# The planner of a two-layer hybrid decoder kernel gets other prices and other ranks

## Chip, core and metric

The kernel runs on one core of a Trainium2 chip. The metric is device time in microseconds for one execution of the whole kernel. Times are compared as medians of several runs; a profiled execution has a span (first to last instruction) and a time of its own that is a little longer than the span.

## What is computed

Two decoder layers over 256 tokens of width 1024, all in float32. Each layer has a projection into six blocks of 512 columns, two kinds of attention (eight plain causal heads, four differential heads), an output projection, and a gated feed-forward of width 2816. A conditioning vector c gives shifts, scales and gates for both halves of the layer.

```python
for l in range(DEPTH):
    mod = (cond @ w_mod[l] + b_mod[l])[:, None, :]
    sh_a, sc_a, g_a, sh_f, sc_f, g_f = jnp.split(mod, N_MOD, axis=-1)
    h = rms_norm(x, norm_mix[l]) * (1 + sc_a) + sh_a
    proj = h @ w_in[l]
    mq, mk, mv, dq, dk, dv = jnp.split(proj, splits, axis=-1)
    ...
    x = x + g_a * (jnp.concatenate([o_m, o_d], axis=-1) @ w_out[l])
    h = rms_norm(x, norm_ffn[l]) * (1 + sc_f) + sh_f
    x = x + g_f * ((jax.nn.silu(h @ w_gate[l]) * (h @ w_up[l])) @ w_down[l])
return x
```

The dots leave out the QK norm, the partial rotary embedding, the two attentions and the norm of their heads.

## The kernel before

The 256 tokens are two row tiles of 128. Each dense product in float32 is made of three products in the rounded type fp32r: an operand is split into hi (rounded) and lo (the rest), and `mm3` adds hi x hi, hi x lo and lo x hi into one PSUM tile (L473 to L475). There are 784 such triples of 128x512, 2352 products.

Weights come from HBM into three buffers `raw` of 1 MB by `load_view`; `split` then makes hi on ScalarE (L463) and lo on VectorE (L464), one pair for each half of a buffer, and when lo of both halves is done the buffer is free for the next load. The modulation weights w_mod (8 MB in two sections for the start, 4 MB for each later section) go another way: `mod_section` loads blocks of 512 KB into two buffers `rawm`, and VectorE multiplies each by its column of c and adds it up (L513); after eight blocks the sum is split (L517, L518), TensorE adds it over the partitions with a matrix of ones (L524, L525), and the row goes to SBUF (L530, L533).

The stages follow one another: the start of layer 0 (`start_layer0`: w_mod for shift and scale, of which TensorE takes a part of the blocks in L923 and VectorE the rest in L926, and the first dense products by column blocks as the normalized input becomes known), attention, output projection, `residual` and `norm_modulate` (L566 to L575: scale, shift, transposes L569, hT), feed-forward in 11 chunks (`GateUp`: products, silu and gate L1077 and L1078, transposes L1079, copies L1086 and L1088 into oT; `Down`: product with w_down), then the same for layer 1. The modulation sections of later stages are worked on beside the dense products.

All loads are issued on SP's queue. The order of each engine's instructions isn't written by hand and isn't left to the framework: `Plan` collects every operation with an engine, a cost in ns and its dependencies, and `schedule` simulates the engines and takes, at each step, the instruction that can start first. Among those that can start within a short window of each other on one engine it takes the one with the highest sum of `tail` (the longest path of costs and latencies behind it) and `boost` (a constant of its kind in `TUNE`, plus its rank). `RANK` holds one number for each call of `mark` (each load, split, modulation step, score and so on), times 10 ns. A buffer is given out in the order in which the planner reaches the load. The order so found is emitted as it stands, and on the chip each engine runs its own queue in that order, waiting on semaphores.

The prices that the planner works with are constants of `Plan` and small functions:

- `DMA_ISSUE` 475 ns on SP's queue, `DMA_SETUP` 650, then bytes by `c_dma` at 335 bytes per ns, one load after another, then `DMA_DONE` until an engine can use the data (910 for ScalarE, 1000 for VectorE, 1180 for TensorE).
- `c_sm(n)`, 108 + 1.042 n, for a small VectorE step of n columns, and `SAME`, 127, between dependent steps of VectorE.
- `c_mm(512, 3)`, 3 x 233, for a triple, and `SWITCH`, 85, added to the first triple after other work on TensorE. A transpose costs 109.
- `pe_run` slows TensorE to half speed where the planner believes that it had been idle.

Of the kernel before, what the change touches and what calls it, by code (L numbers as in the profile page):

```python
# [52 lines left out]
class Op:  # L53
    __slots__ = ("eng", "cost", "fn", "deps", "succ", "left", "bufs", "tail", "boost", "idx", "ready", "end", "start", "soft", "main", "group")


class Plan:
# [119 lines left out]
    def schedule(self):  # L177
# [26 lines left out]
        while len(order) < n:  # L204
            best = None
            for e, lst in avail.items():
                cand, tmin = [], 1e18
                for o in lst:
                    t = max(now[e], o.ready)
                    if e == SP:  # L210
                        t = max(t, dma_free - self.AHEAD)
# [45 lines left out]
            if e == SP:  # L257
                now[e] = t + self.DMA_ISSUE
# [39 lines left out]
def c_sm(n):  # L298
    return 108.0 + 1.042 * n


def c_dma(nbytes):
    return nbytes / 335.0
# [13 lines left out]
    "start": (1678,),  # L317
    "smod": (5423, -57, 14, -70, -18, 43, 0, 0, 155, 117, -1394, 257, -1082,),
    "shead": (46, 804, -76, -532, 594,),
    "load": (47, -56, -395, 30, 28, 71, -86, 35, -22, -2708, 746, -967, 12425, 2019, 5536, 3202, 329, 227, -48, 31,  # L320
# [9 lines left out]
    "split": (-691, -30, -11, -339, -5426, 0, -153, -5503, 1328, 0, -571, 1385, 14, 123, -732, -943, -1544, -955,  # L330
# [863 lines left out]
```

## Time and profile before

| | us |
|---|---|
| median of 3 runs | 709.39 |
| lowest, highest | 708.60, 710.76 |
| the profiled execution, its own time | 709.06 |
| its span | 706.9 |
| TensorE busy | 666.8 |
| VectorE busy | 528.5 |
| ScalarE busy | 391.2 |

Busy time of TensorE is the time in which at least one product is under way; products overlap in the pipeline, so the mean duration of one (about 400 ns) is longer than the distance from one to the next (about 232 ns). The busy share is a mean over stages with different limits, so the profile is read by stretches: for each, TensorE's busy time beside its length, the granted clock, and what the other engines and the loads were doing.

### The profile page before, as it was taken

What the parts mean: (1) busy time and instruction counts of PE and PEld (TensorE: products, weight loads), DVE (VectorE), ACT (ScalarE), POOL (GpSimd) and SP (SyncE); (2) the same over time, 40 slices, a digit from 0 to 9 for tenths busy, and PEclk for the clock granted to TensorE, in tenths of its full rate; (3) what the DMA queues carried; (4) which work ended last, traced back from release to release, by engine and by line L of the source; (5) the groups of instructions that cost most, each with busy time, mean ns of one, the idle gap of its engine ahead of it and who ended that gap; (6) DMA issues with size and microseconds to landing.
All of it is one profiled execution on the core that took longest, in us unless ns stands there. A gap on an engine that the chain in (4) does not pass through costs nothing.

```text
span 706.9 us, 8834 instructions
## 1 busy us (share of the span) xinstructions
PE 666.8 (94%) x3085; PEld 520.7 (74%) x3085; DVE 528.5 (75%) x846; ACT 391.2 (55%) x836; POOL 17.0 (2%) x37
## 2 busy tenths in 40 slices
PE   2988999997999999999989999999999999999997
PEld 1656767775778887878768886788788888888885
DVE  3979899999886778787778998996886554464433
ACT  5335899755454544453345766998755444544420
POOL 2000020000000000000000000000000000000000
PEclk9999999999899999999999999999999999999999
DMA  8988885656678679888883589453537555555501
GB/s 267 346 279 296 314 304 178 219 168 227 221 252 284 230 264 313 304 315 295 268 290 134 192 295 318 175 190 110 179 119 249 188 187 194 194 179 178 179 1 59
DMA packets 92496, 158.25 MB, mean 224 GB/s; under 512 B 6030, under 2 KB 62234, under 8 KB 92452
## 3 DMA queue, kind: packets, MB, share of 16 engines
q1 hardware_dynamic: 92452, 157.69, 65.4%
q8 instruction: 24, 0.39, 0.2%
q14 instruction: 20, 0.16, 0.1%
HBM read 156.62 MB, written 1.05 MB: 223 GB/s over the span
## 4 chain that ended last, share of the span: by engine, by line
PE 56%; DMA 14%; issue 12%; DVE 11%; ACT 4%; SPq 1%; POOL 1%; DVEq 0%; ACTq 0%; POOLq 0%
PE ps L475 16%; PE ps L473 16%; PE ps L474 16%; DMA rawm<-in_w_mod_dram 7%; DVE acc L513 4%; DVE lo L464 3%; DMA raw<-in_w_mod_dram 3%; DMA raw<-in_w_in_dram 2%; ACT hi L463 2%; PE ps L674 2%; PE ps L923 1%; PE ps L735 1%; PE ps L1079 1%; ACT w L609 1%; DMA raw<-in_w_down_dram 1%
## 5 line engine op out<-in xcount | busy, mean ns | idle before, releaser
L464 DVE TENSOR_TENSOR lo<-raw,hi 128x1024 fp32r<-128x1024 f32 (+1 forms) x192 | 230.6, 1210 | 99.7 <-ACT hi L463 99.2
L463 ACT ACTIVATE hi<-raw 128x1024 fp32r<-128x1024 f32 (+1 forms) x192 | 198.9, 1050 | 170.8 <-PE ps L475 119.1
L473 PE MATMUL ps<-hi,hThi 128*128 128x512 f32 x544 | 224.0, 412 | 1.9 <-ACT w L609 1.3
L475 PE MATMUL ps<-hi,hTlo 128*128 128x512 f32 x544 | 216.8, 398 | 0.0
L474 PE MATMUL ps<-lo,hThi 128*128 128x512 f32 x544 | 216.5, 398 | 0.0
L473 PEld LDWEIGHTS ps<-hi,hThi 128*128 128x128 f32 x544 | 103.5, 190 | 27.2 <-issue 1.4
L475 PEld LDWEIGHTS ps<-hi,hTlo 128*128 128x128 f32 x544 | 103.0, 189 | 25.6 <-DVE hTlo L951 0.7
L474 PEld LDWEIGHTS ps<-lo,hThi 128*128 128x128 f32 x544 | 103.5, 190 | 24.9 <-issue 1.4
L513 DVE SCALAR_TENSOR_TENSOR acc<-rawm,cs,acc 128x1024 f32<-128x1024 f32 x80 | 102.5, 1281 | 21.5 <-DMA rawm<-in_w_mod_dram 18.7
L473 PE MATMUL ps<-hi,oThi 128*128 128x512 f32 x240 | 96.7, 403 | 3.1 <-ACT oThi L1086 2.3
L474 PE MATMUL ps<-lo,oThi 128*128 128x512 f32 x240 | 95.7, 399 | 1.6 <-DVE lo L464 1.6
L475 PE MATMUL ps<-hi,oTlo 128*128 128x512 f32 x240 | 95.8, 399 | 1.0 <-DVE oTlo L1088 0.8
L473 PEld LDWEIGHTS ps<-hi,oThi 128*128 128x128 f32 x240 | 45.4, 189 | 13.9 <-ACT oThi L1086 2.8
L474 PEld LDWEIGHTS ps<-lo,oThi 128*128 128x128 f32 x240 | 45.4, 189 | 13.4 <-DVE lo L464 3.2
L475 PEld LDWEIGHTS ps<-hi,oTlo 128*128 128x128 f32 x240 | 45.3, 189 | 12.7 <-DVE oTlo L1088 1.2
L692 ACT ACTIVATE w<-ps,sm,sm 128x128 f32<-128x128 f32 (+1 forms) x64 | 32.6, 530 | 7.0 <-DVE sm L687 7.0
L1077 ACT ACTIVATE w<-ps 128x256 f32<-128x256 f32 x44 | 16.7, 382 | 24.0 <-PE ps L475 23.8
L923 PE MATMUL ps<-raw,w 128*128 128x512 f32 (+1 forms) x26 | 14.4, 690 | 14.8 <-DMA raw<-in_w_mod_dram 14.8
L1078 DVE TENSOR_TENSOR w<-w,ps 128x256 f32<-128x256 f32 x44 | 18.1, 416 | 6.1 <-ACT w L1077 6.1
L552 ACT ACTIVATE w<-xs 128x512 f32<-128x512 f32 x16 | 10.0, 627 | 20.9 <-DVE xs L782 19.1
L926 DVE SCALAR_TENSOR_TENSOR acc<-raw,cs,acc 128x512 f32<-128x512 f32 (+1 forms) x27 | 17.0, 630 | 5.6 <-ACT hi L463 4.1
L1086 ACT ACTIVATE oThi<-ps 128x512 fp32r<-128x512 f32 x22 | 12.5, 592 | 15.1 <-PE ps L1079 15.1
(138 smaller groups left out, 593.1 us busy)
## 6 DMA issues: line engine op xcount, KB each, us to landing
rawm<-in_w_mod_dram SPq DMA_DIRECT2D x80, 512.0 KB
raw<-in_w_gate_dram SPq DMA_DIRECT2D x44, 512.0 KB
raw<-in_w_up_dram SPq DMA_DIRECT2D x44, 512.0 KB
raw<-in_w_down_dram SPq DMA_DIRECT2D x22, 1024.0 KB
raw<-in_w_in_dram SPq DMA_DIRECT2D x18, 1024.0 KB
raw<-in_w_mod_dram SPq DMA_DIRECT2D x32, 256.0 KB
raw<-in_w_out_dram SPq DMA_DIRECT2D x8, 1024.0 KB
raw<-in_w_in_dram SPq DMA_DIRECT2D x4, 768.0 KB
```

What stands on the lines that cost most here:

```text
L463: op(ACT, c_act(n, False), lambda: S.activation(hi[:, :n], raw[:, sl], AF.Copy), [raw], [hi], boost=boost)
L464: op(DVE, c_tt(n), lambda: V.tensor_tensor(lo[:, :n], raw[:, sl], hi[:, :n].bitcast(F32), op=ALU.subtract), [raw, hi], [lo], boost=boost)
L473: TE.matmul(ps[:, :], hi[:, k, tt], w[0][:, sl], start=start, stop=False)
L474: TE.matmul(ps[:, :], hi[:, k, tt], w[1][:, sl], start=False, stop=False)
L475: TE.matmul(ps[:, :], lo[:, k, tt], w[0][:, sl], start=False, stop=stop)
L513: op(DVE, c_stt(D), lambda raw=raw, t=t: V.scalar_tensor_tensor(acc[:, :], raw[:, :], cs[:, t : t + 1], acc[:, :], op0=ALU.mult, op1=ALU.a ...
L674: TE.matmul(pss[par][:, c], q, k, start=True, stop=False)
L692: op(ACT, c_act(n, True, 3), lambda ps=ps, pr=pr, j=j, c=c: S.activation(pr[:, j * n : (j + 1) * n], ps[:, j * n : (j + 1) * n], AF.Exp, b ...
L923: op(PE, 4 * W2 / 2.4 + 4.0, lambda r=r, t=t, ps=ps, W2=W2: TE.matmul(ps[:, :W2], cb[:, t * P : (t + 1) * P], r(), start=t == 0, stop=Fals ...
L926: op(DVE, c_stt(W2), lambda r=r, t=t, av=av: V.scalar_tensor_tensor(av(), r(), cs[:, t : t + 1], av(), op0=ALU.mult, op1=ALU.add), rk + [c ...
L1077: last_silu = op(ACT, c_act(FC), lambda: S.activation(sil[:, :FC], ps[:, :FC], AF.Silu), [ps], [sil], after=silu_set, boost=B)
L1078: op(DVE, c_tt(FC), lambda: V.tensor_tensor(sil[:, :FC], sil[:, :FC], ps[:, FC:], op=ALU.mult), [sil, ps], [sil], boost=B)
```

## The change

Prices of the planner change, and all ranks are replaced. What is computed, the instructions, their shapes and the buffers are those of before; `TUNE` is untouched.

```diff
-    SWITCH = 85.0
-    DMA_ISSUE, DMA_SETUP = 475.0, 650.0
-    DMA_DONE = {ACT: 910.0, DVE: 1000.0, POOL: 1000.0, PE: 1180.0, SP: 1000.0}
+    SWITCH = 4.0
+    DMA_ISSUE, POOL_ISSUE, DMA_SETUP = 475.0, 1000.0, 650.0
+    DMA_DONE = {ACT: 1190.0, DVE: 1280.0, POOL: 1280.0, PE: 1460.0, SP: 1280.0}
...
-        if a.eng == SP:
+        if a.dma:
             return self.DMA_DONE[b.eng]
...
-    def op(self, eng, cost, fn, r=(), w=(), after=(), boost=0.0, main=False, rel=0.0):
+    def op(self, eng, cost, fn, r=(), w=(), after=(), boost=0.0, main=False, rel=0.0, dma=False):
         o = Op()
+        o.dma = dma or eng == SP
...
-            if e == SP:
-                now[e] = t + self.DMA_ISSUE
+            if o.dma:
+                now[e] = t + (self.DMA_ISSUE if e == SP else self.POOL_ISSUE)
...
 def c_sm(n):
-    return 108.0 + 1.042 * n
+    return 70.0 + 1.042 * n
...
-def c_dma(nbytes):
-    return nbytes / 335.0
+def c_dma(nbytes, run=4096):
+
+    return nbytes / (317.0 if run >= 1024 else 300.0)
...
 RANK = {
-    "start": (1678,),
-    "smod": (5423, -57, 14, -70, -18, 43, 0, 0, 155, 117, -1394, 257, -1082,),
+    "start": (-248,),
+    "smod": (5813, 213, 3074, 125, -118, 49, -6, 23, 2, 25, -288, 9, 43,),
...
-    def dma(dst, src, nbytes, w, boost=0.0, **kw):
-        return op(SP, c_dma(nbytes), lambda: nc.sync.dma_start(dst(), src, **kw), w=w, boost=boost)
+    def dma(dst, src, nbytes, w, boost=0.0, q=SP, **kw):
+        eng = nc.sync if q == SP else G
+        return op(q, c_dma(nbytes, 4 * src.shape[-1]), lambda: eng.dma_start(dst(), src, **kw), w=w, boost=boost, dma=True)
...
-    def load_view(parts, tag="raw", boost=0.0):
+    def load_view(parts, tag="raw", boost=0.0, q=SP):
```

Every other entry of `RANK` gets a new value in the same manner. The argument `q` can name GpSimd's queue; no call passes it.

## Rows read from the trace of the kernel before

**Rows 1.** The busy line of the page: busy microseconds, share of the span and instructions of each engine.

```profile
PE 666.8 (94%) x3085; PEld 520.7 (74%) x3085; DVE 528.5 (75%) x846; ACT 391.2 (55%) x836; POOL 17.0 (2%) x37
```

**Rows 2.** The table of busy time by stretch. Columns: the stretch in us from the start of the span, its length, busy time (and instructions) of TensorE's matmuls (PE), its weight loads (PEld), VectorE, ScalarE and GpSimd, the granted TensorE clock as a share of full speed, the busy share of the DMA engines and what they moved in GB/s.

```profile
0.00:11.30 11.30, 0.00 (x0) 0.00 (x0) 0.62 (x4) 8.62 (x18) 4.37 (x23) 1.00 0.78 238
11.30:20.00 8.70, 6.12 (x13) 3.82 (x14) 7.20 (x23) 1.90 (x5) 0.00 (x0) 1.00 1.09 334
20.00:46.00 26.00, 26.00 (x96) 17.66 (x96) 23.70 (x49) 7.83 (x12) 0.95 (x1) 1.00 0.94 308
46.00:62.00 16.00, 13.19 (x49) 8.76 (x47) 12.33 (x40) 8.16 (x12) 0.49 (x1) 1.00 0.96 328
62.00:76.00 14.00, 12.09 (x47) 8.87 (x48) 13.96 (x21) 10.36 (x37) 0.46 (x1) 0.88 0.72 251
76.00:96.00 20.00, 17.42 (x81) 13.22 (x80) 16.82 (x49) 18.01 (x96) 0.62 (x3) 1.00 0.92 326
96.00:129.00 33.00, 33.00 (x197) 23.73 (x197) 31.20 (x75) 30.18 (x105) 3.44 (x3) 1.00 0.50 187
129.00:158.00 29.00, 27.60 (x167) 21.87 (x166) 26.23 (x46) 18.98 (x45) 0.96 (x1) 1.00 0.67 222
158.00:181.00 23.00, 16.93 (x73) 12.07 (x72) 22.02 (x37) 10.89 (x20) 0.95 (x1) 0.92 0.68 224
181.00:201.00 20.00, 20.00 (x86) 16.16 (x85) 17.18 (x24) 11.94 (x20) 0.00 (x0) 0.92 0.62 210
201.00:282.00 81.00, 78.66 (x345) 62.68 (x344) 61.46 (x62) 38.34 (x47) 1.85 (x2) 1.00 0.83 278
282.00:360.00 78.00, 78.00 (x345) 62.58 (x344) 59.58 (x59) 32.79 (x40) 1.02 (x2) 1.00 0.86 299
360.00:368.00 8.00, 4.92 (x17) 3.42 (x16) 5.87 (x9) 5.38 (x8) 0.00 (x0) 0.82 0.76 266
368.00:440.00 72.00, 72.00 (x352) 56.38 (x351) 65.16 (x114) 42.90 (x76) 0.96 (x1) 1.00 0.68 237
440.00:512.00 72.00, 70.48 (x395) 56.36 (x394) 61.67 (x126) 64.32 (x204) 0.96 (x1) 1.00 0.49 165
512.00:698.00 186.00, 186.00 (x825) 149.93 (x824) 97.79 (x110) 80.57 (x103) 0.00 (x0) 1.00 0.47 159
698.00:707.00 9.00, 4.39 (x19) 3.19 (x17) 5.71 (x10) 0.00 (x0) 0.00 (x0) 0.97 0.32 117
```

**Rows 3.** The waits of TensorE over the span: line, who was waited for, us in total, times, the longest.

```profile
PE ps L923 <- DMA raw<-in_w_mod_dram: 14.8, 3, 11.4
PE ps L569 <- DVE w L568: 3.1, 3, 1.6
PE ps L473 <- ACT oThi L1086: 2.3, 1, 2.3
```

**Rows 4.** The timeline of TensorE around 48 us: start, duration, what; in brackets the idle time ahead of it and what ended it.

```profile
46.73 0.40 PE L475 MATMUL ps<-hi,hTlo 128*128 128x512 f32 x1
49.38 1.10 PE L923 MATMUL ps<-raw,w 128*128 128x512 f32 x2 [2.26 <-DMA raw<-in_w_mod_dram]
```

**Rows 5.** The timelines of ScalarE and of TensorE around 362 us.

```profile
361.36 1.06 ACT L463 ACTIVATE hi<-raw 128x1024 fp32r<-128x1024 f32 x1 [4.67 <-DMA raw<-in_w_in_dram]
362.32 1.07 ACT L1086 ACTIVATE oThi<-ps 128x512 fp32r<-128x512 f32 x2
...
363.44 0.50 PE L473 MATMUL ps<-hi,oThi 128*128 128x512 f32 x1 [2.33 <-ACT oThi L1086]
...
364.93 0.67 PE L475 MATMUL ps<-hi,oTlo 128*128 128x512 f32 x1 [0.75 <-DVE oTlo L1088]
```

**Rows 6.** The timelines of VectorE and of TensorE ahead of the feed-forward of layer 0.

```profile
169.15 2.60 DVE L513 SCALAR_TENSOR_TENSOR acc<-rawm,cs,acc 128x1024 f32<-128x1024 f32 x2
...
173.07 1.22 DVE L518 TENSOR_TENSOR lo<-acc,hi 128x1024 fp32r<-128x1024 f32 x1
...
174.34 0.50 PE L525 MATMUL ps<-lo,onesr 128*128 128x512 f32 x1 [0.88 <-DVE lo L518]
...
176.85 0.67 PE L569 MATMUL ps<-ident,w 128*128 128x128 f32 x4 [1.55 <-DVE w L568]
```

**Rows 7.** The chain that ended last, in order of time, at a load of 512 KB (rawm) and at one of 1 MB (raw): start, us, what. A DMA's piece goes from the start of its issue to its landing.

```profile
316.82 4.05 DMA rawm<-in_w_mod_dram
...
320.96 1.30 DVE acc L513
...
353.96 7.30 DMA raw<-in_w_in_dram
```

**Rows 8.** The timeline of VectorE in the chain of small steps that works out the rotary angles.

```profile
41.38 0.17 DVE L830 TENSOR_SCALAR kk<-kk 128x16 f32<-128x16 f32 x1
41.59 0.17 DVE L830 TENSOR_SCALAR kp<-kk 128x16 f32<-128x16 f32 x1
```

**Rows 9.** The timeline of TensorE at a change from transposes to dense products.

```profile
75.05 0.63 PE L635 MATMUL ps<-ident,w 128*128 128x128 f32 x4
...
75.76 0.40 PE L474 MATMUL ps<-lo,hThi 128*128 128x512 f32 x1
```

**Rows 10.** The waits of SP's DMA queue, the longest in total.

```profile
SPq L445 <- DVE lo L464: 232.5, 74, 11.7
```

More of the change, by code (lines that the diff above doesn't have):

```diff
@@ L53 @@
 class Op:
-    __slots__ = ("eng", "cost", "fn", "deps", "succ", "left", "bufs", "tail", "boost", "idx", "ready", "end", "start", "soft", "main", "group")
+    __slots__ = ("eng", "cost", "fn", "deps", "succ", "left", "bufs", "tail", "boost", "idx", "ready", "end", "start", "soft", "main", "group", "dma")
 class Plan:
@@ L256, in schedule @@
             now[e] = o.end
-            if e == SP:
-                now[e] = t + self.DMA_ISSUE
+            if o.dma:
+                now[e] = t + (self.DMA_ISSUE if e == SP else self.POOL_ISSUE)
                 o.start = max(dma_free, now[e] + self.DMA_SETUP)
@@ L316 @@
 RANK = {
-    "start": (1678,),
-    "smod": (5423, -57, 14, -70, -18, 43, 0, 0, 155, 117, -1394, 257, -1082,),
-    "shead": (46, 804, -76, -532, 594,),
-    "load": (47, -56, -395, 30, 28, 71, -86, 35, -22, -2708, 746, -967, 12425, 2019, 5536, 3202, 329, 227, -48, 31,
[9 rows of a table removed]
-    "split": (-691, -30, -11, -339, -5426, 0, -153, -5503, 1328, 0, -571, 1385, 14, 123, -732, -943, -1544, -955,
[10 rows of a table removed]
-    "small": (-304,),
-    "qk": (928, 3661, 760, 0, 7233, -353, 4129, 3658, 702, 929, -890, -1288, 9623, 5514, 155, -394,),
@@ L343 @@
-    "values": (1089, -1436, 3482, 0, 1556, -7, -621, 487,),
-    "mod": (10322, 1598, -5442, 198, -193, 816, -230, 5198, 1421, 1919, 283, 2809, -1051, 0, 2321, 7399, 3936, 2059,
[4 rows of a table removed]
-    "modsum": (2277, 4704, 1864, -3911, -443, 4744, -653, -14, 147, 1773,),
-    "score": (4283, 58, -257, -333, -15, -6337, 152, 432, 293, 4213, -4410, -2953,),
-    "prob": (-35, -201, 1641, -113, 1944, 3659, 146, 84, -143, -318, 3, -868, -71, 410, 10714, -23, -45, -58, 902,
-        11377, 0, 1047, -1861, 417,),
-    "rinv": (-1382, 261, 2495, 6769, -10687, 962, 1196, -8714,),
@@ L354 @@
-    "mix": (1272, 3309, 3414, -2657, 816, 105,),
-    "pv": (88, -7274, -1224, 0, -123, 7533, 1679, 4514, 11886, 1854, 1086, 15, -282, 0, 0, 3090, 4491, 79,),
-    "heads": (5698, 3641, -8, 368, 4959, -366, 1408, 2441,),
-    "res": (-213, -587, 117, -103, 9218, 1018, 39, 12, 4975, -3920, -956, -791, 3869, 8797, 1178, 7200,),
-    "xrstd": (-56, 0, 14519, 6442, 1231, -118,),
-    "norm": (819, -246, 1218, -623, 1220, 68, 94, -26, 1575, 582, 2087, 338,),
-    "act": (28, -161, -2267, -1044, -802, -916, -1046, 250, -794, -1883, -4067, -50, -14260, 1668, -3233, -2995, 40,
-        1, 1575, 157, 601, -20, 2292, 86, 468, 1893, -517, 1547, 0, 1044, 1175, -902, -1651, -1853, -245, 7341, 51,
-        -3985, 135, -1337, 0, 42, -5464, -5439,),
@@ L363 @@
-    "aT": (4485, 534, -10757, -2641, -1038, -13578, -1638, 473, -6665, 3494, 59, -2558, 418, -2716, -28, -248, 4611,
-        84, -1742, -4170, 1329, -4036,),
+    "start": (-248,),
+    "smod": (5813, 213, 3074, 125, -118, 49, -6, 23, 2, 25, -288, 9, 43,),
+    "shead": (283, 209, 311, -884, 748,),
+    "load": (2488, 5618, 321, 3574, -272, -6, -16, 4487, 0, -22, 483, -494, -16, -57, -324, 98, 154, 185, 38, 96,
[9 rows of a table added]
+    "split": (-3533, -218, 102, -5748, 769, -2824, -5328, -1257, 857, -4222, 1064, -174, 2440, 135, -811, -5217,
[10 rows of a table added]
@@ new lines @@
+    "small": (871,),
+    "qk": (-35, 1954, -85, 18, 15, -219, 2316, 1451, 100, 102, 430, 7387, 1339, -3, 6502, 1497,),
+    "values": (202, 51, -177, 1313, -368, -430, 9117, 3485,),
+    "mod": (6906, 1964, 4710, -860, 120, -1031, 75, 4770, 257, -341, 4972, 30, 447, 4370, 983, 1521, 1783, -206,
[4 rows of a table added]
+    "modsum": (170, 24, 401, -2450, 3247, 4421, -168, -28, -350, 2257,),
+    "score": (2969, -22, -36, 154, 45, -1373, 85, -93, 302, 1237, 3040, -27,),
+    "prob": (-268, 132, -14, 51, -13, 33, -15, 48, -30, -29, -71, -45, -1307, -353, 1745, -841, -144, -150, 5590,
+        736, -288, 408, 1597, -30,),
@@ new lines @@
+    "rinv": (918, -352, 3806, 166, 3655, -3767, 108, 350,),
+    "mix": (7838, 402, 776, -61, 3603, 2320,),
+    "pv": (4, 191, -101, 564, 1427, 3028, 68, 3751, 7239, 698, 2207, -519, 61, 5530, 0, 4246, 6054, 5933,),
+    "heads": (-13, -34, 53, -7, 562, 1708, 3223, 604,),
+    "res": (87, 53, 434, 16, 3796, -1654, -57, 3, 3103, 14268, -406, -491, 530, -1238, -2020, -194,),
+    "xrstd": (16, 157, -6554, 3884, 2621, -149,),
+    "norm": (15163, 650, 204, 0, 0, 0, 3761, -243, 2948, 2739, 4574, 3681,),
@@ L365 @@
+    "act": (-118, 179, 1116, -1229, 4936, 6541, -74, -1137, 430, 3540, 2566, -7642, 3669, 1372, 2779, 255, -955,
[4 rows of a table added]
 }
@@ L454, in load_view @@
         for key, view, src, nbytes in parts:
-            dma(lambda view=view: view(raw.tile), src, nbytes, [(raw, key)], boost=boost)
+            dma(lambda view=view: view(raw.tile), src, nbytes, [(raw, key)], boost=boost, q=q)
         return raw
```

50 rows, old and new, of the table RANK are left out of this document.

## The prediction

> **What bounds the kernel now.** I read the busy line of the page first: TensorE is busy 666.8 us (94% of the span of 706.9), VectorE 528.5 [rows 1]. So TensorE bounds the whole, and as the change adds and removes no instruction, the most that a new order could win is the 40.1 us in which TensorE stands still, plus what it loses at the lower clock.
>
> The table of busy time by stretch says where those microseconds lie [rows 2]. The reader should look at three columns in each row: TensorE's busy time against the length, the granted clock, and whether VectorE or the load stream is full in the same stretch. Three long stretches show TensorE busy all the time at clock 1.00: 282 to 360, 368 to 440 and 512 to 698, together 336 us; nothing is to be won there. The first 20 us lose 13.9 (11.3 + 2.6) before and between the first loads, and the last 9 lose 4.6 behind the last product; I count both as fixed. What is left is a pool of short stalls:
>
> (a) 46 to 76: 2.81 + 1.91 idle, and the clock of 0.88 over 14 us costs 0.12 x 14 = 1.7: 6.4 in all.
> (b) 76 to 96: 2.58 idle.
> (c) 129 to 201: 1.40 + 6.07 idle, and 0.92 over 23 and over 20 us costs 1.8 + 1.6: 10.9.
> (d) 201 to 282 and 440 to 512: 2.34 + 1.52 = 3.9 idle, thinly spread over 153 us.
> (e) 360 to 368: 3.08 idle, and 0.82 over 8 us costs 1.4: 4.5.
>
> The pool is 28.3 us. The clock's two levels are 2.4 and 1.2 GHz; the stretches below 1.00 are those in which TensorE had just stood still, so their loss goes when the stall goes.
>
> Then the waits of TensorE, for what ended each stall, and the timeline around the three largest. The waits name a load (14.8 us, 11.4 of it the very first), the normalized rows w of L568, and oThi of L1086 [rows 3]. In (a) the last dense product before the gap starts at 46.73 and the next work waits 2.26 us for a block of w_mod [rows 4], while the stream already runs at 308 to 328 GB/s [rows 2]. In (e) ScalarE reaches the split of a w_in load before its bytes are there, stands 4.67 us, and the copy L1086 that TensorE needs is queued behind it: TensorE waits 2.33 and then 0.75 [rows 5]. In (c) VectorE is busy 22.02 of 23 us; two modulation sums L513 and the split L518 lie ahead of the row of shifts, and TensorE's transposes L569 wait 1.55 us for it [rows 6].
>
> **The change, part by part.** No duration on the chip is altered: prices only decide in which order the planner writes each engine's queue and which buffer a load gets. So each price is worth what its error did to the order.
>
> Loads. The old price of a 512 KB load that waits for its buffer is 475 issue + 650 setup + 524288/335 = 1565 + 1000 until VectorE: 3.69 us. The new one is 475 + 650 + 1654 + 1280 = 4.06. The trace has such a load start at 316.82 and VectorE start on it at 320.96: 4.14 [rows 7]. The new price is 0.08 short, the old 0.45. For 1 MB into ScalarE the old sum is 475 + 650 + 3130 + 910 = 5.17, the new 5.62; the w_in load of (e) took 7.30 from 353.96 [rows 7], behind others. So the new price closes 0.46 of an error of 2.1. In the start it is the rate that counts: 238 x 11.3 + 334 x 8.7 + 308 x 26 = 13.6 MB by 46 us [rows 2]; that is 40.6 us at 335 bytes per ns and 42.9 at 317. The difference, 2.3, is the size of the 2.26 us stall at 49.38. So the old planner did not see that stall and the new one does.
>
> One rule of the Trainium skill speaks against the higher load price: DMA: Bandwidth & Descriptors, section "Anatomy of one DMA", puts the fixed part of a load on GpSimd's path at about 2.0 us. With 1.65 for 512 KB at 317 that would be 3.65, the old price, and the raise would only put work off. The 4.14 us of [rows 7] stand against it.
>
> Small VectorE steps. Their price for 16 columns falls from 108 + 17 = 125 to 87 ns, with 127 between dependent ones: 252 before, 214 now. The chain of the rotary angles starts a step every 0.21 us [rows 8]. The new price fits within 4 ns. It frees 38 ns a step in the plan and nothing on the chip; where VectorE is full, as in (c), the planner now sees some room that it did not use.
>
> First dense product after other work (SWITCH 85 to 4). Four transposes at 109 and one product at 233 are 669 ns; with 85 it is 754, with 4 it is 673. The trace has 0.71 us from the first transpose at 75.05 to the second product at 75.76 [rows 9]: 0.04 over the new price, 0.04 under the old. Nothing hangs on it.
>
> The choice of a GpSimd queue for loads has no caller that passes it; every load stays on SP's queue, so GpSimd's queue is not used more and its issue price of 1000 ns is idle. Cost nil, and no cover is needed.
>
> The new ranks are the part without a row: they change nearly every choice between ready instructions. I bound them by stage. Nothing recovered is 0; everything recovered is the pool; and in the three full stretches they can only lose. One late load there costs what it costs in (e), 4.5 us with its clock.
>
> What I take: (a) 2.0 of 6.4: the bytes are the same and the stream is full until 62 us, so only work that the load does not hold can move into the gap. (b) 0.5 of 2.6: loads at 326 GB/s and ScalarE at 18.0 of 20 both hold [rows 2]. (c) 2.5 of 10.9: VectorE has only 1.8 + 2.8 + 1.0 = 5.6 us of idle between 96 and 181 [rows 2], and about half of that should be usable, since its sums wait on loads that are now priced right. (d) 0.5 of 3.9. (e) 2.0 of 4.5, for the reason that the mispriced load is its cause, though the price closes only a part. New stalls in the full stretches: 1.5 lost. Sum: -2.0 - 0.5 - 2.5 - 0.5 - 2.0 + 1.5 = -6.0. The profiled execution took 709.06 (span 706.9 and 2.16 around it), 0.33 under the median of 709.39; 709.06 - 6.0 = 703.1, or 703.4 as a median. Late after the change: in (a) the same load stream, in (c) VectorE, so neither goes to zero.
>
> **The rivals.** First, no change: the limits in (a) to (c) are a full load stream and a full VectorE, which no order widens. The stalls then move, and (d) and (e) give about 1 us that new ones take back: 709. For it: 22.02 of 23 and 328 GB/s. Against: the full stretches show that the planner can keep TensorE fed wherever its prices hold, and (e) is not such a limit. Chance 0.16.
>
> Second, slower, by the raw buffers. Believing in later loads, the planner ranks other work ahead of the splits; ScalarE and VectorE then take a landed load later, its buffer comes free later, and the next load is issued later: SP's queue already waits 232.5 us in total for VectorE's L464 to free a buffer [rows 10]. In the layer-0 feed-forward (201 to 360) the stream runs at 278 and 299 GB/s [rows 2], so a slip is not caught up at once and ends as a stall like (e). The terms (a) to (e) give 7.5; two such stalls (9.0) outweigh them, and that is the point from which it decides; three make 13.5 - 7.5 = +6: 715. For it: only three raw buffers. Against: VectorE is busy just 61.5 of 81 and 59.6 of 78 us there, so splits need not wait long. Chance 0.15.
>
> Third, much more: with stalls seen in advance, half the pool goes and none is added: 709.06 - 14 = 695. For it: each stall is short and other dense work follows within 1 to 3 us. Against: (c). Chance 0.10.
>
> Fourth, the higher load price is wrong: then (a) and (e) give nothing, 709.06 - 3.5 + 1.5 = 707.1. A load of 3.7 us in a quiet stream would show it; the nearest I have is 4.14. Chance 0.05. By the rule of the Trainium skill's page DMA: Bandwidth & Descriptors this would be the outcome.
>
> **How the numbers follow.** A measurement of this kernel can tell about 0.3%, so "the same" is 707.3 to 711.5. My forecast, 698 to 707.3 with 703 as the likeliest, has 0.54. With the third rival, faster has 0.64. The first and the fourth make 0.21 for the same, and slower is 0.15. The range for 8 in 10 leaves out half of the third rival below and most of the second above: 696 to 712.
>
> **What would show it.** Right: at 360 to 368 ScalarE no longer stands in front of L1086 and the clock stays at 1.00 there; the gap before 49.38 is shorter than 1 us or has dense products in it; 158 to 201 stays at clock 1.00 while VectorE is still over 95% busy; the three full stretches stay full. Wrong: TensorE's idle time (40.1 us) is the same or more with stalls at new places, above all with a raw load as releaser between 201 and 360; or the start is shortened by far more than 2 us, which would mean that it was not the load stream that held it.

## The result, and the profile after

The changed kernel took 699.3 us (median of 4 runs, 698.36 to 700.71), the kernel before 710.08 beside it (4 runs, 708.6 to 711.08). The ratio is 0.9851, with a 95% interval of 0.9825 to 0.9878. The forecast was 703.0, with a range of 696 to 712. The profiled execution of after took 698.36 with a span of 696.2, against 709.06 and 706.9 before: 10.7 us less on either. The lines named here stand three lower than before (L473 to L475 are L476 to L478 now).

The busy line of the page of after (answers to [rows 1]):

```profile
PE 663.0 (95%) x3085; PEld 519.3 (75%) x3085; DVE 528.1 (76%) x846; ACT 391.5 (56%) x836; POOL 16.8 (2%) x37
```

The instructions are the same in number on every engine, and the busy time of VectorE and ScalarE has hardly moved. TensorE's busy time fell by 3.8 us (666.8 to 663.0) with the same 3085 instructions, and its idle time from 40.1 to 33.2 (696.2 - 663.0).

The table of busy time by stretch of after (answers to [rows 2], same columns; the stretches past 350 are set by after's own stages):

```profile
46.00:62.00 16.00, 15.65 (x63) 10.80 (x62) 13.60 (x39) 7.64 (x12) 0.95 (x1) 1.00 1.02 370
62.00:76.00 14.00, 13.25 (x58) 10.25 (x57) 13.60 (x31) 12.31 (x63) 0.00 (x0) 1.00 0.74 248
76.00:96.00 20.00, 19.52 (x110) 15.02 (x109) 18.49 (x50) 18.22 (x75) 2.87 (x4) 1.00 0.99 347
96.00:129.00 33.00, 29.21 (x160) 20.97 (x158) 30.71 (x72) 27.04 (x94) 0.95 (x1) 0.90 0.56 189
...
158.00:181.00 23.00, 18.31 (x73) 13.26 (x72) 21.98 (x35) 11.32 (x22) 0.95 (x1) 0.93 0.65 229
181.00:201.00 20.00, 20.00 (x92) 16.19 (x91) 19.18 (x27) 11.92 (x17) 0.00 (x0) 1.00 0.69 225
201.00:282.00 81.00, 80.46 (x356) 64.23 (x355) 64.62 (x64) 38.04 (x46) 1.91 (x2) 1.00 0.86 296
282.00:350.00 68.00, 67.61 (x296) 53.79 (x295) 51.80 (x52) 30.61 (x37) 0.95 (x1) 1.00 0.86 300
350.00:360.00 10.00, 10.00 (x48) 8.06 (x47) 8.66 (x11) 6.58 (x9) 0.00 (x0) 1.00 0.88 320
360.00:430.00 70.00, 70.00 (x335) 55.93 (x334) 61.21 (x111) 43.86 (x74) 1.91 (x2) 1.00 0.62 206
...
502.00:688.00 186.00, 186.00 (x825) 149.85 (x825) 97.54 (x110) 80.92 (x103) 0.00 (x0) 1.00 0.47 159
```

TensorE's column is now almost full in 46 to 96, and the place of the old stall (e) is full at clock 1.00. But one stretch that was full before, 96 to 129, has lost 3.8 us and some clock.

The waits of TensorE in after, over the span (answers to [rows 3]):

```profile
PE ps L926 <- DMA raw<-in_w_mod_dram: 11.3, 1, 11.3
PE ps L931 <- DVE acc L929: 4.3, 2, 3.9
PE ps L572 <- DVE w L571: 3.2, 3, 1.7
PE ps L638 <- ACT w L630: 1.8, 1, 1.8
PE ps L527 <- ACT w L630: 1.2, 1, 1.2
```

TensorE waits for a load once instead of three times, 11.3 us instead of 14.8, and the wait for oThi is gone. In the start VectorE's sums took over: TensorE waits 4.3 us for acc of L929, so that at the first dense product after is only 0.6 us ahead. It waits for the rows w of L571 as before (3.2 and 3.1 us): that is the full VectorE of (c). New are two waits for ScalarE's w of L630, in attention. The timeline of TensorE there (start, duration, then in brackets the idle time before it and its releaser):

```profile
106.30 0.50 PE L527 MATMUL ps<-hi,onesr 128*128 128x512 f32 x1 [1.20 <-ACT w L630]
...
108.85 1.12 PE L638 MATMUL ps<-ident,w 128*128 128x128 f32 x4 [1.81 <-ACT w L630]
...
110.74 0.79 PE L476 MATMUL ps<-hi,hThi 128*128 128x512 f32 x1 [0.78 <-ACT qkT L641]
```

ScalarE works there through the 16 short squares of the keys' norm (L612, about 0.2 us each) while the PSUM tiles of the keys are held, and TensorE has no other tile to go on with: 1.20 + 1.81 + 0.78 = 3.8 us idle. The clock falls behind it:

```profile
107.70:114.53 6.83, 4.91 (x16) 3.82 (x16) 6.50 (x14) 4.73 (x17) 0.00 (x0) 0.50 0.34 103
```

The planner knew of this stall. The schedule that the planner of after makes (model times) has TensorE idle there for 1.19, 2.05 and 0.94 us, 4.2 in all, between the triples 79 and 80; only the clock at half speed isn't in it. The two stalls of before at 49.38 and in (e) are of the other kind: the old planner's schedule has no idle time of TensorE over 0.3 us there, while the stalls of (c) are in it, with up to 1.85 us each.

ScalarE and SP's queue at the former stall (e), timeline of after (answers to [rows 5]; first ScalarE, then two loads of w_in, and the second of them by itself):

```profile
353.24 1.06 ACT L466 ACTIVATE hi<-raw 128x1024 fp32r<-128x1024 f32 x1 [1.73 <-PE ps L478]
354.20 0.58 ACT L1089 ACTIVATE oThi<-ps 128x512 fp32r<-128x512 f32 x1
...
356.55 0.59 ACT L1089 ACTIVATE oThi<-ps 128x512 fp32r<-128x512 f32 x1
357.03 1.06 ACT L466 ACTIVATE hi<-raw 128x1024 fp32r<-128x1024 f32 x1
```

```profile
344.54 3.02 SPq L448 DMA_DIRECT2D raw<-in_w_in_dram  x2
...
347.19 0.38 SPq L448 DMA_DIRECT2D raw<-in_w_in_dram  x1
```

The split that stood in front of the copies before is the one at 357.03 here, and its load is the second of the two: by the order in which the kernel emits loads and splits, the one at 344.54 belongs to the split at 353.24. So the load that was issued at 353.96 before [rows 7] is issued at 347.19. The split between the copies finds its bytes there, and no L1089 stands behind a load.

Where the 10.7 us came from can be counted by the dense triples, which run in one fixed sequence in both kernels. The start of a triple's first product, before and after (other work of TensorE can move across such a mark, so a part is good to about 1 us; between the marks 96 and 150 a second profiled execution of after, that of after_again, takes 1.6 us longer than this one):

```
triple      0      48     64     80     96     150    200    350    376    392    520    783
before   22.36  75.44  89.96 110.77 136.71 197.98 235.32 347.38 372.17 384.25 510.48 701.53
after    21.78  71.94  85.25 110.74 136.86 194.41 230.76 343.24 362.34 374.52 499.87 690.87
diff     -0.58  -3.49  -4.70  -0.03  +0.15  -3.57  -4.56  -4.14  -9.82  -9.73 -10.61 -10.67
```

So (a) gave 3.5 us (0.6 of it ahead of the first triple), (b) 1.2, the new stall in attention cost 4.85 (from -4.70 to +0.15), (c) gave 3.7 (to triple 150; 2.1 by after_again), (e) 5.6 (from -4.14 to -9.73), and the stretches of (d) 0.6 and 0.9.

### The profile page after: what moved, and what is told of

It is laid out like the page before. It is cut to its first block, busy times and chain, and to the rows that moved or that the text cites. A ratio compares the mean times of both kernels' runs of the same rounds, so it can differ in the third digit from the quotient of the medians.

```text
span 696.2 us, 8830 instructions
## 1 busy us (share of the span) xinstructions
PE 663.0 (95%) x3085; PEld 519.3 (75%) x3085; DVE 528.1 (76%) x846; ACT 391.5 (56%) x836; POOL 16.8 (2%) x37
## 4 chain that ended last, share of the span: by engine, by line
PE 64%; DMA 14%; DVE 12%; ACT 6%; issue 2%; SPq 1%; POOL 0%; DVEq 0%; ACTq 0%; POOLq 0%
PE ps L477 19%; PE ps L478 19%; PE ps L476 19%; DMA rawm<-in_w_mod_dram 6%; DMA raw<-in_w_mod_dram 3%; DVE acc L516 3%; DVE lo L467 3%; PE ps L738 2%; ACT hi L466 1%; ACT w L612 1%; DMA raw<-in_w_in_dram 1%; DVE acc L929 1%; PE ps L677 1%; PE ps L1082 1%; DMA raw<-in_w_out_dram 1%
## 5 line engine op out<-in xcount | busy, mean ns | idle before, releaser
L467 DVE TENSOR_TENSOR lo<-raw,hi 128x1024 fp32r<-128x1024 f32 x192 | 230.7, 1210 | 97.8 <-ACT hi L466 96.9
L466 ACT ACTIVATE hi<-raw 128x1024 fp32r<-128x1024 f32 x192 | 199.1, 1052 | 153.3 <-PE ps L478 111.9
L476 PE MATMUL ps<-hi,hThi 128*128 128x512 f32 x544 | 222.9, 410 | 1.9 <-ACT hThi L952 1.2
L478 PE MATMUL ps<-hi,hTlo 128*128 128x512 f32 x544 | 216.8, 398 | 0.1
L476 PEld LDWEIGHTS ps<-hi,hThi 128*128 128x128 f32 x544 | 103.2, 190 | 26.9 <-ACT hThi L952 1.7
L478 PEld LDWEIGHTS ps<-hi,hTlo 128*128 128x128 f32 x544 | 103.0, 189 | 24.8 <-DVE hTlo L954 0.5
L476 PE MATMUL ps<-hi,oThi 128*128 128x512 f32 x240 | 97.3, 405 | 1.5 <-ACT oThi L769 0.8
L478 PE MATMUL ps<-hi,oTlo 128*128 128x512 f32 x240 | 95.2, 397 | 0.3 <-DVE oTlo L771 0.3
L476 PEld LDWEIGHTS ps<-hi,oThi 128*128 128x128 f32 x240 | 45.2, 188 | 11.6 <-ACT oThi L769 1.0
L478 PEld LDWEIGHTS ps<-hi,oTlo 128*128 128x128 f32 x240 | 45.1, 188 | 11.3 <-DVE oTlo L771 0.7
L926 PE MATMUL ps<-raw,w 128*128 128x512 f32 (+1 forms) x26 | 13.4, 646 | 11.3 <-DMA raw<-in_w_mod_dram 11.3
L929 DVE SCALAR_TENSOR_TENSOR acc<-raw,cs,acc 128x512 f32<-128x512 f32 (+1 forms) x27 | 16.9, 631 | 5.0 <-DMA raw<-in_w_mod_dram 4.4
L677 PE MATMUL ps<-qkT,qkT 64*128 64x128 f32 (+1 forms) x128 | 19.1, 375 | 0.5 <-ACT qkT L641 0.5
```

The source lines that it names most:

```text
L466: op(ACT, c_act(n, False), lambda: S.activation(hi[:, :n], raw[:, sl], AF.Copy), [raw], [hi], boost=boost)
L467: op(DVE, c_tt(n), lambda: V.tensor_tensor(lo[:, :n], raw[:, sl], hi[:, :n].bitcast(F32), op=ALU.subtract), [raw, hi], [lo], boost=boost)
L476: TE.matmul(ps[:, :], hi[:, k, tt], w[0][:, sl], start=start, stop=False)
L478: TE.matmul(ps[:, :], lo[:, k, tt], w[0][:, sl], start=False, stop=stop)
L677: TE.matmul(pss[par][:, c], q, k, start=True, stop=False)
L929: op(DVE, c_stt(W2), lambda r=r, t=t, av=av: V.scalar_tensor_tensor(av(), r(), cs[:, t : t + 1], av(), op0=ALU.mult, op1=ALU.add), rk + [c ...
```

## The experiments

The theory, called L in the expectations, from the profile: the old planner believed loads to be there sooner than they are, so its order ran into stalls that it didn't see; with the new load prices the search sees and removes them, and the load prices do most of the work. The rivals: that any long new search would do as well, whatever the prices; that the small steps and SWITCH do it; and, beside these, that the new load price isn't the duration of a load at all (the prediction's fourth rival).

Except in the two load tests the whole reference is computed. New ranks of my own come from a random search: change some ranks, make the planner's order again, keep it if the planner's end falls. Each is the outcome of one such search; how far two searches with the same prices differ was not measured.

**1. loads_alone.** It leaves out the whole computation and only loads. One buffer is loaded and read, then loaded again; then streams with nothing to wait for, in rows of 4 KB, 2 KB, 1 KB and 512 B.

```diff
+            for t in range(KT):
+                nc.sync.dma_start(one[:, :1024], wm[:, t, s * D : (s + 1) * D])
+                V.scalar_tensor_tensor(acc[:, :], one[:, :1024], cs[:, t : t + 1], acc[:, :], op0=ALU.mult, op1=ALU.add)
+        for k in range(10):
+            ...
+            nc.sync.dma_start(one[:, :].rearrange("p (a b) -> p a b", b=512), wi[:, 4 * g : 4 * g + 4, ...])
+            S.activation(hi[:, :], one[:, :], AF.Copy)
```

> Leaves out the whole computation; it only loads weights. Part 1 loads 512 KB into one buffer, which VectorE reads before the next load; part 2 the same with 1 MB and ScalarE; part 3 streams 8 MB each in rows of 4 KB, 2 KB, 1 KB and 512 bytes with nothing to wait for. By the new prices a 512 KB load lies between two VectorE steps for 475 + 650 + 1654 + 1280 = 4.06 us and a 1 MB load between two ScalarE steps for 5.62 us, and the streams run at 317 GB/s (300 for 512 bytes). By the old prices 3.69 and 5.17 us, and 335 GB/s for all. By the Trainium skill's page DMA: Bandwidth & Descriptors, section Anatomy of one DMA, the fixed part would be 2.0 us, and so 512 KB 3.6 us (an estimate with the rate of the stream).

The timeline of VectorE and ScalarE in it: the bracket is the whole time from the end of one read, which frees the buffer, to the start of the next.

```profile
12.71 1.28 DVE L88 SCALAR_TENSOR_TENSOR acc<-one,cs,acc 128x1024 f32<-128x1024 f32 x1 [3.39 <-DMA one<-in_w_mod_dram]
17.41 1.28 DVE L88 SCALAR_TENSOR_TENSOR acc<-one,cs,acc 128x1024 f32<-128x1024 f32 x1 [3.42 <-DMA one<-in_w_mod_dram]
...
100.69 1.91 ACT L93 ACTIVATE hi<-one 128x2048 fp32r<-128x2048 f32 x1 [5.08 <-DMA one<-in_w_in_dram]
107.70 1.91 ACT L93 ACTIVATE hi<-one 128x2048 fp32r<-128x2048 f32 x1 [5.10 <-DMA one<-in_w_in_dram]
```

The table by stretch for the four streams (columns here: stretch, length, VectorE, ScalarE, GpSimd, clock, DMA share, GB/s):

```profile
151.00:166.00 15.00, 0.00 (x0) 1.14 (x1) 0.00 (x0) 1.00 1.03 410
168.00:185.00 17.00, 0.18 (x1) 0.00 (x0) 0.00 (x0) 1.00 1.05 389
187.00:206.00 19.00, 0.35 (x2) 0.00 (x0) 0.00 (x0) 1.00 0.88 293
208.00:240.00 32.00, 0.35 (x2) 0.00 (x0) 0.00 (x0) 1.00 1.03 282
```

A lone load of 512 KB takes 3.4 us from free buffer to VectorE, one of 1 MB 5.1 us to ScalarE. The old prices say 3.69 and 5.17, the new ones 4.06 and 5.62: for a load by itself the old prices are the nearer. From first to last packet the streams run at 403, 369, 337 and 286 GB/s (the table's stretches lie inside the streams, but the third begins before its stream). 524288 bytes at 403 bytes per ns are 1.3 us, which leaves 2.1 us fixed. The fixed part of about 2.0 us in the Trainium skill (DMA: Bandwidth & Descriptors, "Anatomy of one DMA") agrees with this, though the page gives it for GpSimd's path and these loads are on SP's queue.

**2. loads_busy.** It leaves out the computation too: the same serial loads of 512 KB while nothing else, ScalarE, VectorE, TensorE or all three work without pause, then two streams beside all three.

```diff
+        for busy in ((0, 0, 0), (1, 0, 0), (0, 1, 0), (0, 0, 1), (1, 1, 1)):
+            phase(*busy, 34.0, serial)      # 8 loads into one buffer
+        phase(1, 1, 1, 28.0, rows4k)
+        phase(1, 1, 1, 30.0, rows1k)
```

> Leaves out the whole computation. Eight loads of 512 KB follow one another into one buffer, in five phases: alone; while ScalarE copies 128x1024 tiles without a break; while VectorE subtracts such tiles; while TensorE multiplies; with all three. Then 8 MB stream in rows of 4 KB and of 1 KB with all three at work. If busy engines slow the loads, the distance from load to load rises from about 3.4 us towards the 4.06 of the new price and the streams fall from 404 and 342 GB/s to about 320. If they don't, all stays as alone (within 0.1 us and 3%), and the late loads of the whole kernel come from loads queued behind each other.

SP's queue in it (start of the first issue, time to the end of the last of eight), while ScalarE, VectorE, TensorE and all three work:

```profile
33.74 25.38 SPq L96 DMA_DIRECT2D one<-in_w_mod_dram  x8
...
62.36 25.44 SPq L96 DMA_DIRECT2D one<-in_w_mod_dram  x8
...
90.94 26.01 SPq L96 DMA_DIRECT2D one<-in_w_mod_dram  x8
...
120.17 25.32 SPq L96 DMA_DIRECT2D one<-in_w_mod_dram  x8
```

Less the last issue itself (0.33), seven spacings in 25.32 to 26.01 us are 3.57 to 3.67 us each, whichever engine works; in the quiet phase, once the loads ahead of it are done, they are 3.45 to 3.59. In the last phase ScalarE joins only at 128.20, behind the third issue; the spacings from there on are 3.49 to 3.61. The stream of 4 KB rows still issues a load every 1.28 us beside three busy engines (524288 / 1.28 = 410 bytes per ns). So busy engines make a load some 0.1 us longer at most in the mean. In the whole kernel loads are late where other loads are ahead of them. Of the rawm loads of before for which VectorE stood still, one issued at 147.01, 1.8 us behind another rawm load, reached VectorE 4.85 us later; two issued at 322.27 and 416.09, 3.2 and 2.3 us behind a raw load, 5.60 and 5.48; one at 129.70, 1.3 us behind a raw load, 6.10; and one at 289.87, with two raw loads less than 3 us ahead, 7.60. With nothing issued in the 5 us ahead the trace of before has this one, 3.28 us from issue to VectorE:

```profile
230.60 0.34 SPq L445 DMA_DIRECT2D rawm<-in_w_mod_dram  x1
...
233.88 1.28 DVE L513 SCALAR_TENSOR_TENSOR acc<-rawm,cs,acc 128x1024 f32<-128x1024 f32 x1 [1.04 <-DMA rawm<-in_w_mod_dram]
```

After has another at 472.08: 3.30 us. The 4.14 us of [rows 7], on which the prediction leaned, was thus not a quiet load: a raw load had been issued 4.6 us ahead of it. The new price of 4.06 us is a quiet load and some 0.7 us more.

**3. swap_one_split.** The kernel before, with nothing but the w_in split of (e) moved behind the copies that were queued behind it, on ScalarE and VectorE.

```diff
+    late = [o for o in order if o.group == ("split", 102) and o.eng != PE]
+    last = next(o for o in order if o.group == ("aT", 10) and o.eng == DVE)
+    order = [o for o in order if o not in late]
+    at = order.index(last) + 1
+    order[at:at] = late
```

> The kernel before with one change: one half-split of a layer-1 w_in load (ScalarE's copy and VectorE's rest) is emitted behind the copies L1086 and L1088 of the last feed-forward chunk of layer 0 instead of ahead of them. If the stall at 360 to 368 comes from that split standing in front of L1086 while its load is late, TensorE's waits of 2.33 and 0.75 us and the lower clock (1.4 us) go: 4.5 us less, ratio about 0.9935. If the triples there would wait for another thing as well, or the time comes back in layer 1, the ratio is 0.998 to 1.002.

707.57 us (12 runs) against 709.12 (23 runs); ratio 0.9989, 0.9961 to 1.0016. ScalarE's timeline there, the stretch of (e) and the one after it, and what TensorE waited for in the latter:

```profile
352.81 1.09 ACT L1086 ACTIVATE oThi<-ps 128x512 fp32r<-128x512 f32 x2 [3.11 <-PE ps L1079]
...
357.33 2.00 ACT L463 ACTIVATE hi<-raw 128x1024 fp32r<-128x1024 f32 x2
```

```profile
356.00:364.00 8.00, 6.88 (x31) 5.30 (x31) 5.81 (x6) 3.31 (x4) 0.00 (x0) 1.00 0.64 218
364.00:384.00 20.00, 18.75 (x85) 14.85 (x84) 18.42 (x32) 11.86 (x22) 0.00 (x0) 1.00 0.52 180
```

```profile
372.37 0.66 PE L569 MATMUL ps<-ident,w 128*128 128x128 f32 x4 [1.25 <-DVE w L568]
```

The stall did go: the copies run first, the clock stays at 1.00, and from triple 350 to 376 the profiled execution gains 3.65 us on that of before. By triple 392 it has given back 1.5: TensorE waits 1.25 us for VectorE's rows w of L568, while no product waits for the moved split. (This execution, 700.78 us, is the fastest of the twelve, and 5.95 us ahead of before already at triple 350, which the change doesn't touch.) Over the whole run no gain is shown clear of noise, and 0.9935 lies outside the interval. After did something else: against the triples around it the load is issued 2.6 us earlier and ScalarE reaches the split 4.5 us later.

**4. new_prices_old_ranks and old_prices_new_ranks.** One part of the change each.

```diff
 RANK = {
-    "start": (-248,),
+    "start": (1678,),
...
```

(all ranks of before under the new prices; the other kernel is the reverse, the kernel before with after's `RANK`).

> All new prices, ranks of before. Theory L (the gain comes from ranks that were found with prices at which late loads are seen): no gain, since these ranks were fitted to other prices; 706 to 716 us. Theory P (right prices put the work in a better order by themselves): most of the gain, 699 to 705 us.

> All old prices, the new ranks. Theory L: the ranks fit the prices with which they were found, and are worse than nothing without them; 715 us or more, since nearly every choice is then another one. Theory S (the new ranks are better numbers, whatever the prices): 699 to 705 us.

New prices with old ranks: 710.87 us (10 runs), ratio 1.002 (0.999 to 1.005). Old prices with new ranks: 746.32 us (4 runs), 1.0521 (1.0478 to 1.0565). Both came out as theory L expected, and neither part alone gives anything. Ranks are offsets to a choice that the prices make; these were worth something only under the prices they came with.

**5. search_all_new, search_load_price, search_small_and_switch.** My own search, 60,000 trials from the ranks of before, under all the new prices, the new load prices alone, and the new small-step and SWITCH prices alone. The same search under all old prices found nothing better than the 691.6 that the old planner gives before's order (model time; there is no run of it).

```diff
 RANK = {
-    "start": (1678,),
+    "start": (28179,),
...
```

> All new prices; ranks from a search of my own that starts at the ranks of before (60,000 trials). Replayed with the new prices its order ends at 694.4 us, with the old ones at 706.2; the order of before ends at 705.1 with the new and 691.6 with the old ones. Theory L (the new prices, the load's above all, tell the chip's time of an order): 1.8 to 8 us over 694.4 as seen in the two known traces, and 2.1 around the span: 698 to 705 us, a gain. If the old prices were the right ones: about 14 us slower than before, 723 us.

> Only the load prices are new (SWITCH 85 and the small-step price as before); ranks from the same search with the same number of trials, from the ranks of before. Replayed with all new prices its order ends at 702.9 us, with the old ones at 705.7. Theory L: 707 to 713 us, about as before, since the search had got no further than this order; if the old prices were right, 722 us. A time under 705 would say that the load price alone carries the gain.

> Only the small-step price and SWITCH are new, the load prices are those of before; ranks from the same search with the same number of trials. The planner that made it expects 698.2 us; replayed with all new prices the order ends at 717.6, with the old ones at 708.0. Theory L: the loads come later than this planner thinks, 721 to 728 us, slower than before and the slowest of the three. If the load price doesn't matter, it is as fast as the search with all new prices, 698 to 705 us.

All new prices: 704.79 us (7 runs) against 709.6 (22 runs), ratio 0.9931 (0.9883 to 0.9979). Load prices alone: 711.95, 1.0043 (1.0015 to 1.007). Small steps and SWITCH alone: 715.11, 1.0076 (1.0041 to 1.011). The first lies in the range that theory L gave it, and so does the second; the third is the slowest, as expected, but not as slow as its range (721 to 728). A search of the same length under all three prices does gain, 0.7%. That the load prices do most of the work isn't shown: alone they are slower than before, by 0.4%, and the small steps and SWITCH alone too. This part of the theory falls.

**6. after_again, search_further, search_late_loads.** On one chip: after itself; its ranks searched on for 48,000 trials with the planner's end as the goal; and its ranks searched for another goal (some 178,000 trials): the mean end of six replays of the order in which each load comes late by a random time (0.5 us in the mean, at most 1.5) and the phase of the planner's model of the slow clock is shifted. Only `RANK` differs.

```diff
 RANK = {
-    "start": (-248,),
+    "start": (6729,),
...
```

(that of search_late_loads; search_further has 14511.)

> The changed kernel as it is, timed again beside the next two on one chip. Its order ends at 688.2 us in the planner; if each load lands late by a random part of 1.5 us (mean 0.5) and the clock's phase is shifted, the mean of six replays is 705.1. Measured before: 699.3.

> The ranks after, searched further with the same prices and the same goal (the planner's end, 48,000 trials): 687.9 us in the planner, 702.1 as the mean of the six replays with late loads. If the planner's end tells the chip's time to a few tenths, 699.0 us; if what is left is how an order bears late loads, 696 to 700 us.

> The ranks after, searched with the same prices but another goal: the mean of the six replays in which each load lands late by a random part of 1.5 us. The planner's end is 688.0 us, as good as the search further; the mean of the replays is 691.6, 10.5 less. Theory L carried further (what costs time on the chip is loads that land later than planned, and orders differ in how they bear it): 692 to 697 us, clearly under the other two. If prices alone matter: 699 us, the same as the search further.

Against 708.31 us for before (7 runs): after 698.76, 0.9859 (0.9818 to 0.99); search_further 698.12, 0.9854 (0.9821 to 0.9886); search_late_loads 693.07, 0.9783 (0.9746 to 0.9821). More search for the planner's end brings nothing. The search for orders that bear late loads brings another 5.7 us (693.07 against 698.76), though its planned end, 688.0, is that of after, 688.2, within 0.2. Its busy line and two stretches:

```profile
PE 659.1 (95%) x3085; PEld 519.2 (75%) x3085; DVE 528.9 (77%) x846; ACT 391.8 (57%) x836; POOL 16.2 (2%) x37
```

```profile
96.00:129.00 33.00, 32.58 (x190) 24.17 (x189) 31.54 (x72) 28.86 (x99) 0.95 (x1) 1.00 0.64 214
...
282.00:360.00 78.00, 78.00 (x348) 62.88 (x347) 61.95 (x63) 36.45 (x46) 0.95 (x1) 1.00 0.87 295
```

Attention (96 to 129) is almost full again, at clock 1.00: the stall that after had newly made is not there. Half of what this kernel gains over before is busy time of TensorE, 666.8 to 659.1.

**7. old_prices_late_loads.** The same goal under all old prices (some 183,000 trials from the ranks of before): the kernel before with another `RANK`, nothing else.

```diff
 RANK = {
-    "start": (1678,),
+    "start": (29669,),
...
```

> All prices of before; ranks searched from those of before with the goal of the late loads (the mean of six replays in which each load lands late by a random part of 1.5 us). With the old prices its order ends at 692.0 us, 0.4 later than the order of before (691.6). Replayed with the new prices it ends at 696.0, where the order of before ends at 705.1. If late loads are what costs time, and an order that bears them will do without right prices: 700 to 706 us, a gain of 4 to 9. If right prices are needed: 708 to 711 us, as before.

692.89 us (4 runs) against 708.66 (7 runs), ratio 0.9792 (0.9732 to 0.9852): as fast as search_late_loads, and below every number that was expected of it. So the new prices are not needed for a gain of this size. Its busy line, the waits of TensorE, and those of VectorE and ScalarE for loads:

```profile
PE 660.6 (96%) x3085; PEld 518.4 (75%) x3085; DVE 526.9 (76%) x846; ACT 390.9 (57%) x836; POOL 16.7 (2%) x37
```

```profile
PE ps L896 <- DMA raw<-in_w_mod_dram: 12.8, 3, 10.9
PE ps L446 <- ACT w L582: 1.6, 1, 1.6
```

```profile
ACT hi L436 <- DMA raw<-in_w_up_dram: 28.4, 15, 3.6
...
DVE acc L486 <- DMA rawm<-in_w_mod_dram: 18.6, 21, 3.2
```

VectorE still stands 21 times for a rawm load, 18.6 us in all, exactly the count of before (21 times, 18.7), and the longest wait is longer. Yet past the start TensorE has no wait for a load among its largest. So VectorE finds its loads late as often as before, and TensorE hardly stands for it; that other work is ready for it then is my reading, which no run tests by itself.

The planner's replay puts the orders side by side. Each order is kept as it was emitted and simulated with either set of prices, and with the new prices and late loads (mean of six replays); these three are model times (the random draws are others than those behind the figures in the expectations), the last column is the chip's median.

```
order                      old prices  new prices  new + late   chip
before                        691.6       705.1       722.1     708.3 to 710.1
after                         700.4       688.2       705.2     699.3
new_prices_old_ranks          714.8       705.2       718.0     710.9
old_prices_new_ranks          740.5       753.6       766.5     746.3
search_all_new                706.2       694.4       707.2     704.8
search_load_price             705.7       702.9       716.3     712.0
search_small_and_switch       708.0       717.6       732.6     715.1
search_further                698.8       687.9       703.9     698.1
search_late_loads             695.7       688.0       692.7     693.1
old_prices_late_loads         692.0       696.0       705.4     692.9
```

Read down the first column: the old planner calls before's order the best of all, and after's 8.8 us longer. The second column puts most of the kernels in the chip's order. With old prices the replay of before's order is at 355.35 us when triple 376 starts, with new prices at 369.35; the chip has 372.17. But this doesn't show that the new prices are the better ones: the first column does as well once before's own row is left out, and it has after at 700.4 (chip 699.3), search_all_new at 706.2 (704.8) and search_further at 698.8 (698.1), where the new prices have 688.2, 694.4 and 687.9. What falls short by 10 to 18 us is the end that a planner gives to an order that was searched for that very end: before by the old prices, those three by the new ones, and search_small_and_switch, 698.2 by its own prices and 715.1 on the chip. Such a search picks, among others, the orders about which its prices are too hopeful; a goal with random lateness leaves less of that. This fits all rows but search_load_price (705.5 by its own prices, 712.0); no run tests it by itself. The last row is in line with it: 696.0 by the new prices, more than after's 688.2, and 692.9 on the chip, less than after's 699.3. For before's order the load prices alone give 707.7 in the replay, where all new prices give 705.1 and all old ones 691.6; the small steps alone give 692.6, SWITCH alone 690.5. The loads are the part that matters in the replay.

## Why the prediction was right, and where its sizes were off

The direction and the bound were right: the gain came out of the pool of short stalls (40.1 us idle before, 33.2 after), the stretches from 282 on that were full stayed full but for 0.39 us, and nothing in the instructions changed. The predicted time is 3.7 us above the measured one and the range holds it. Term by term:

| term | predicted | measured | |
|---|---|---|---|
| (a) 46 to 76 | -2.0 | -3.5 | idle 4.72 to 1.10, clock 1.00; 0.6 of it lies ahead of the first triple |
| (b) 76 to 96 | -0.5 | -1.2 | idle 2.58 to 0.48, at 347 GB/s instead of 326 |
| (c) 129 to 201 | -2.5 | -3.7 | TensorE still waits for w of L571, 2.5 us there; -2.1 by after_again |
| (d) | -0.5 | -1.5 | |
| (e) | -2.0 | -5.6 | the whole stall and its clock |
| new stalls | +1.5 | +4.85 | in attention, not in a stretch that was counted; +4.1 by after_again |
| sum | -6.0 | -10.65 | |

**The step that was mis-sized most is (e).** It took 2.0 of 4.5 because "the price closes only a part": 0.46 of an error of 2.1 us. That reasoning treats a price as if it repaired its own error in place. But the new order doesn't shift the load by the change of its price. Counted from triple 350, the load is issued 2.6 us earlier (347.19 against 353.96, in a kernel that runs 4.1 us ahead there) and ScalarE reaches the split 4.5 us later, 7.1 us in all where 4.67 were missing; so this stall went whole. The error of a price is thus no bound on what a new order wins. swap_one_split shows the other half: removing this stall by hand gives part of it back 16 triples later.

**New stalls** were put in the three full stretches, at 1.5. Those held. The fourth full stretch, 96 to 129 [rows 2], was left out of the list, and there it cost 4.85 us. The mechanism is not that of the second rival: no raw load is the releaser, ScalarE's short steps of the keys' norm are. Nor is it an error of a price: the planner has these 4.2 us of idle time in its own schedule, and the order was kept with them for an earlier end. What it doesn't have is the 6.8 us at half speed behind them, in which TensorE worked for 4.91 us and so lost some 2.5 (an estimate); its schedule of after has triple 80 at 108.29 and triple 96 at 132.46, the chip at 110.74 and 136.86.

**The loads' paragraph** argued that the new price fits (4.06 against 4.14). As a duration of a load by itself this is wrong: 3.4 us. The fourth rival's sign, a load of 3.7 us or less in a quiet stream, stood in the trace of before (3.28 us at 230.60), so that "the nearest I have is 4.14" misread it. The rival's result, 707.1, did not follow. That the price works as an allowance for loads queued behind other loads would explain it, but no run shows it: with the load prices alone the search gained nothing (711.95). The rule of the Trainium skill that was weighed there (DMA: Bandwidth & Descriptors, "Anatomy of one DMA") agrees with the 3.4 us; what was drawn from it for the time of the kernel fell with that rival.

**Signs.** That the stall at 49.38 and that of (e) were unseen by the old planner and went is the part of the mechanism that the traces show; that the load price is what made them go is not shown, since neither half of the change gains alone, nor do the load prices alone, nor the other two. As forecast: ScalarE no longer stands in front of the copies and the clock is 1.00 there; the stall before 49.38 is gone (0.35 us idle in 46 to 62); VectorE is over 95% busy in 158 to 181 (21.98 of 23); the three full stretches stayed full. Not as forecast: 158 to 181 is still at clock 0.93, only 181 to 201 is at 1.00; the start gained 3.5 where about 2 was expected, while the stream ran faster in the same stretch (370 GB/s instead of 328 in 46 to 62), so part of the room there was in the order of the loads and not in the rate of the stream.

**Open.** Whether the late loads or the shifted phase of the clock in the goal makes the last 6 us isn't separated. Nor is it from the number of trials, three times that of the plain searches; only search_further, which stopped gaining, speaks against that. The goal's lateness adds 0.5 us to a load in the mean, so that a 512 KB load at old prices has 3.69 + 0.5 = 4.19 us in it, about the new price: that a spread does more than one raised price is likely from search_late_loads against search_further, but wasn't tried with a fixed 0.5. Why search_load_price is slower than before, with the part that counts most in the replay, is not explained.

The best version is 693 us (search_late_loads, old_prices_late_loads), 2.1 to 2.2% under before and 0.8 to 0.9% under after.

## What to carry to other kernels

What counts of a planner's prices is which order they make it choose. So compare an order's replay with its trace at marks along the way, don't trust the end that a planner gives to an order searched for that end (10 to 18 us short here in most cases), and search the ranks again with every change of price. Search for an order that still holds when loads come late by a random time, not for the lowest planned end: at the same planned end (688) that was worth 5.7 us here. When costing such a change, allow for a stall that goes whole, however small the price's part in it, and charge every stretch that is full now, not only the long ones, for stalls that may come.

## What the runs showed of the hardware that was not expected

A 512 KB load on SP's queue takes 3.4 us alone, and in loads_busy about 3.5 us from load to load with idle engines and 3.6 to 3.7 beside ScalarE, VectorE or TensorE at work: compute hardly slows it, but with loads ahead of it on the same queue it took 4.85 to 7.60 us. A stream of loads runs at 403 GB/s with rows of 4 KB and at 286 with rows of 512 B. A third to a half of what a better order wins is busy time, not idle time: the same 3085 instructions of TensorE took 666.8 us before, 663.0 after and 659.1 in search_late_loads. With stalls, time at the lower clock went too (0.88 to 1.00 in 62 to 76); ahead of the last product TensorE worked for 12.9 us at half speed before, 8.1 after and 9.5 in search_late_loads, which by my estimate is 2.4 and 1.7 us of the 3.8 and 7.7. The rest isn't explained.
